# Attention units transposed in pairs, key copies by DMA, GpSimd's results used a step later

## The chip, the cores and the metric

The kernel runs on one core of a Trainium2 chip. The core has five engines that run their own instruction streams and meet at semaphores: TensorE (matrix products; PE in the profile, PEld for its weight loads), VectorE (DVE), ScalarE (ACT), GpSimd (POOL) and SyncE (SP, which here only issues DMAs). Data moves between the chip's memory (HBM) and the core's memory (SBUF) by DMA; results of TensorE land in PSUM, in banks of 128 x 512 floats.

The metric is the time of one execution on the device in microseconds (us), the median of several runs.

## The reference: what is computed

One layer of an encoder block for 1024 tokens of width 1024.

```
h = x @ w_in                                  # 1024 x 1024 @ 1024 x 3328
q_a,k_a,v_a,z_a,q_b,k_b,v_b,z_b = split(h)
y_a = neighborhood_attention(q_a,k_a,v_a)     # 8 heads, grid 16 x 64, window 8 x 16, learned bias
y_b = windowed_gqa_with_sink(rotary(q_b), rotary(k_b), v_b, sink)   # 8 query heads, 2 key heads, |i-j| <= 128
mixed = concat(y_a * silu(z_a), y_b * silu(z_b))
out = layer_norm(2**0.25 * x + mixed @ w_out)
```

Each head has width 64. Both attentions are a softmax over a small window: scores, exponential, division by the sum, weighted sum of the values.

## The kernel before

Float32 accuracy is made of half-precision matmuls: every operand is split into a high and a low float16 part, and a product is three matmuls (high x high, low x high, high x low). ScalarE makes the high part, VectorE or GpSimd the difference.

**Stages.** A prologue computes the values v and the first six column groups of h. The attention loop follows, and at its end the output product with w_out and the layer norm.

**The attention loop.** There are 128 units of work, each one block of 128 queries of one head: units 0 to 63 belong to group b (a 128-query block of one of 8 heads against up to three key blocks), units 64 to 127 to group a (a tile of the grid against three key pieces). Step i of the loop emits, for unit i, the two score matmuls (`stage_qk`, L816 and L817), the bias, minimum and scale on VectorE (L826) and the exponential on ScalarE (`stage_exp`, L842). For unit i - 1 it emits `stage_tr`: ScalarE writes the high part of the probabilities (L852) and VectorE the low part (L853) into a `split` tile, and SP issues a DMA that transposes it, block by block of 128 x 128, into a `tr` tile (L856). Three key pieces with two parts make 6 blocks; the first and the last query block of a head of group b have two key pieces and 4 blocks. Every four units make a group, whose weighted sums with the values (PV, `stage_pv`, L881) stand at step 4q + 9 for group q, so 5 steps after the transpose of its last unit was emitted. `stage_on` divides by the sums (L890), `stage_ot` transposes the result back (L901).

**What fills TensorE.** Between these the loop pumps matmuls of the remaining projections (`project`, L379) and, later, of the output product (L1031), spread over the steps by the table `FILL_AT`.

**Order and queues.** The order of the loop's instructions is written out by hand. Work that the projections bring along goes into four queues, one for each of ScalarE, VectorE, GpSimd and SP (`enq`, L155 on); each step takes a few operations from each (`pop`). An operation may be taken when the operations that it depends on were emitted at an earlier step; `lag` asks for further steps between, two for a DMA. `need` emits what is still queued when a stage must have it. Weight halves pass through such a chain: load (L188, SP), high part (L199, ScalarE), scale and difference (L204 and L205, GpSimd). Queries of group b are rotated (`rope`: L311, L312, then L313 to L315 on GpSimd) and then cast (L259, ScalarE) and subtracted (L265, GpSimd). Keys are cast (L257), subtracted (L263), and their high and low rows are copied to the other half of the partitions (`split_k`, L295, GpSimd), so that each head's keys stand twice, against the high and the low rows of the queries.

**Buffers.** Six `split` tiles are used in turn; the `tr` pool has nine. The score banks in PSUM are four.

Of the kernel before, what the change touches and what calls it, by code (L numbers as in the profile page):

```python
# [9 lines left out]
F16 = mybir.dt.float16  # L10
I32 = mybir.dt.int32
BF16 = mybir.dt.bfloat16
AF = mybir.ActivationFunctionType
# [11 lines left out]
PSCALE = 2.0 ** 14  # L25
MSCALE = 2.0 ** -44
QSCALE = 2.0 ** -15
LTT, LPP, BP, BH, BR, ND, NA, NX, F1 = 1, 6, 2, 9, 5, 1, 1, 6, 0.2
NSPLIT, NP = 6, 2
ORDER = ["zb0", "z0", "zb1", "kb", "qb0", "z1", "qb1", "zb2", "qb2", "k0", "qb3", "zb3", "q0", "k1", "q1",  # L30
         "k2", "q2", "z2", "k3", "q3", "z3"]
NPRO = 6
# [11 lines left out]
WO_TAG = ("wor", "wor", "raw", "raw") + ("wr",) * 5 + ("wor", "wor", "raw", "raw", "raw", "wr", "wr")  # L44
WO_SCAN = ((9, 2), (12, 4), (10, 6), (13, 8), (14, 10), (15, 13))
WO_PREV = {15: ("s", 9), 0: ("s", 10), 1: ("s", 15), 2: ("s", 12), 3: ("s", 13), 11: ("s", 14)}
WO_SCALE = 55
M_AT = [105, 112, 118, 120]
WO_AT = [67, 71, 75, 79, 84, 88, 93, 98]
WO_LD = [16, 22, 19, 25, 36, 39, 42, 45, 48, 112, 116, 28, 130, 130, 130, 130]  # L50
# [11 lines left out]
def hybrid_block(ctx, tc, xT, x, wt, wv, wo, bias, sink, gain, lbias, cos, sin, bmask, out):  # L62
    nc = tc.nc
# [19 lines left out]
    def big_tile(name, shape=(128, 2, 512), dt=F32R):  # L83
        n = taken[0]
        taken[0] += 1
        tag = "big" if n < 8 or 16 <= n < 24 or n >= 32 + NS else "big2"
        return big.tile(list(shape), dt, tag=tag, name=name)

    xh, xl, x16h, x16l = {}, {}, {}, {}
    for half in range(2):  # L90
        for k in range(KT):
            t = big_tile(f"x{half}{k}", dt=F32 if half else F32R)
# [51 lines left out]
    clock = {"step": None}  # L144

    class Op:
        def __init__(self, eng, fn, deps, prio):
            self.eng, self.fn, self.deps, self.step = eng, fn, [d for d in deps if d is not None], None
            self.prio, self.born, self.lag = prio, clock["step"], 2 if eng == "sp" else 0

        def emit(self):
            self.fn()
# [2 lines left out]
    def enq(eng, fn, *deps, prio=1, after=0):  # L155
        op = Op(eng, fn, deps, prio)
        if clock["step"] is not None:
            queues[eng].append(op)
        elif after:
            events.setdefault(ran[0] + after, []).append(op.emit)  # L160
        else:
            op.emit()
        return op
# [3 lines left out]
    def pop(eng, n, top=1, same=False):  # L167
        q = queues[eng]
        ready = [op for op in q if op.prio <= top and all(
            d.step is not None and d.step + d.lag < clock["step"] + (same and op.prio == 0 and d.eng == "act") for d in op.deps)]  # L170
        for op in sorted(ready, key=lambda op: op.prio)[:n]:
            q.remove(op)
            op.emit()
# [80 lines left out]
    def split_hl(h, l, src, scaled, eng):  # L254
        def hi():
            if scaled:
                nc.scalar.activation(h(), src, AF.Copy, scale=QSCALE)  # L257
            else:
                nc.scalar.copy(h(), src)  # L259

        def lo():
            if scaled:
                nc.vector.scalar_tensor_tensor(l(), src, QSCALE, h(), op0=ALU.mult, op1=ALU.subtract)  # L263
            else:
                (nc.gpsimd if eng == "pool" else nc.vector).tensor_sub(l(), src, h())  # L265

        return hi, lo
# [15 lines left out]
    def split_k(p, half, src, dep=None):  # L283
        sl = slice(512 * half, 512 * half + 512)
        ops = []
        prio = 0 if dep is None else 1
        eng = "pool" if dep and clock["step"] is not None else "dve"
        for j in range(2):
            a, o = slice(64 * j, 64 * j + 64), slice(64 - 64 * j, 128 - 64 * j)
            hi, lo = split_hl(lambda j=j, a=a: own("kh", p, j)[a, sl], lambda j=j, a=a: own("kl", p, j)[a, sl],  # L290
                              src[a], dep is None, eng)

            def dup_(w, j=j, a=a, o=o):
                t = own(w, p, j)
                nc.gpsimd.tensor_copy(t[o, sl], t[a, sl])  # L295

            o1 = enq("act", hi, dep, prio=prio, after=28 if dep else 0)
            o2 = enq(eng, lo, o1, prio=prio, after=32 if dep else 0)
            ops.append(o2)
            dup = [enq("pool", lambda d=dup_: d("kh"), o1, after=32 if dep else 0),  # L300
                   enq("pool", lambda d=dup_: d("kl"), o2, after=36 if dep else 0)]
            stk_ops.setdefault((p, j, half), []).extend(dup)
        return ops

# [420 lines left out]
    ap = actx.enter_context(tc.tile_pool(name="ap", bufs=3, reuse_waits="tile"))  # L725
# [28 lines left out]
        return us  # L754

    units = unit_list()
    split = [ap.tile([128, 3, 2, 128], F16, name=f"split{i}", bufs=1) for i in range(NSPLIT)]
    sns = [ap.tile([128, 388], F32, name=f"sn{i}", bufs=1) for i in range(2)]
    for t in split:
        nc.gpsimd.memset(t, 0.0)  # L760
# [2 lines left out]
    st = {}  # L763
    on = {}

    def geom(u):
        g, p, j, t, _ = u
        if g == "a":
            b, half = t
            w = WINW[b]  # L770
            return NKEY[b], [4 * w] * 3
        lo, hi = max(t - 1, 0), min(t + 2, 8)
        return 128 * (hi - lo), [128] * (hi - lo)
# [69 lines left out]
        st[u, "p"] = pt  # L843

    def stage_tr(u):
        g, p, j, t, _ = u
        n, ch = geom(u)
        pt = st.pop((u, "p"))
        c, m = ch[0], len(ch)
        hl = split[units.index(u) % NSPLIT]  # L850
        src = pt[:, :n].rearrange("p (k c) -> p k c", c=c)
        nc.scalar.activation(hl[:, :m, 0, :c], src, AF.Copy, scale=PSCALE)  # L852
        nc.vector.scalar_tensor_tensor(hl[:, :m, 1, :c], src, PSCALE, hl[:, :m, 0, :c],  # L853
                                       op0=ALU.mult, op1=ALU.subtract)
        tr = ap.tile([128, 6, 128], F16, tag="tr", name="tr", bufs=BH)
        nc.sync.dma_start(tr[:, :2 * m, :], hl[:, :m].rearrange("p k i c -> p (k i c)"), transpose=True)  # L856
        st[u, "tr"] = tr

    def quad(q):
        g, p, j, t, _ = units[4 * q]  # L860
# [320 lines left out]
    for i in range(-LD, NU + LO):  # L1181
        if 0 <= i + LD < NU:
            stage_load(units[i + LD], i)
        if i < 0:
            continue
        clock["step"] = i
        per, h = divmod(i, 16)
        bulk["step"] = i
        if i in VA_AT:
            gather_v(0, VA_AT.index(i))  # L1190
        for n, at_ in WO_SCAN:
            if at_ == i:
                load_ops["wo", ("s", n)] = enq("sp", lambda n=n: wo_load(n, True), wo_ops.get(WO_PREV.get(n) if n == 15 else None))
                wo_scan(n, True)
        for n in range(16):
            if WO_LD[n] == i:
                load_ops["wo", n] = enq("sp", lambda n=n: wo_load(n), wo_ops.get(WO_PREV.get(n) if n < 15 else None),
                                        wo_ops.get({9: 0, 10: 1, 12: 2, 13: 3, 14: 4, 15: 5}.get(n)),
                                        w_ops.get(17 + n if 4 <= n <= 8 else None))
                if n < 9 or n == 11:  # L1200
                    wo_scan(n)
        if i == WO_SCALE:
            wo_scale()
        for n in range(len(WO_AT)):
            if WO_AT[n] == i:
                wo_split(n)
        if i == 131:
            enq("sp", gain_load, *m_ops[4])
        if i in M_AT:
            m_queue(4 + M_AT.index(i))  # L1210
        if bulk["last"] != i or (queues["sp"] and i - queues["sp"][0].born > 2):
            pop("sp", 1 if i < 118 else 3)
        if i < NU:
            u = units[i]
            if u[3] in (0, 4):
                need(*stk_ops[f"b{u[1]}", u[2], u[3] // 4])
            if u[3] == (0, 0):
                need(*stk_ops[u[1], u[2], 0], *stk_ops[u[1], u[2], 1])
            stage_qk(u)
        q, m = divmod(i - LP - 3, 4)  # L1220
        if i >= Q30 + 2:
            q, m = (NU // 4 - 2, i - Q30 - 2) if i < Q30 + 4 else divmod(i - LP - 3, 4)
        elif i >= Q30:
            q, m = -1, 0
        if m == 0 and 0 <= q - 1 < NU // 4:
            stage_ot(q - 1)
        if m == 0 and 0 <= q < NU // 4:
            stage_pv(q)
        if i > Z3_END:
            pop("dve", 1, 0)  # L1230
        if 0 <= i - LT < NU:
            stage_tr(units[i - LT])
        pop("act", 1, 0)
        pump_to(i + F1)
        if 0 <= q < NU // 4:
            g, p, j, h = quad(q)
            if g == "a" and p < 3 and (j, h, m) in VA_STEP:
                gather_v(p + 1, VA_STEP.index((j, h, m)))
        if m == 1 and 0 <= q < NU // 4:
            stage_on(q)  # L1240
        pop("dve", ND if i < M_AT[1] else 2, same=True)
        if i < NU:
            stage_exp(units[i])
        pop("act", NA if i < M_AT[0] and len(queues["act"]) < 5 else 2)
        pop("pool", NP)
        pump_to(i + 1)
# [78 lines left out]
```

## Time and profile before

| | |
|---|---|
| median of 3 runs | 446.06 us (445.18 to 448.8) |
| the profiled execution, its own time | 446.49 us |
| its span from first to last instruction | 444.7 us |
| TensorE busy | 437.5 us, 98% |
| VectorE, ScalarE busy | 344.2 us (77%), 308.3 us (69%) |
| GpSimd busy | 221.6 us (50%) |
| DMA moved | 81.39 MB, 183 GB/s on average |
| transposes issued by SP | 128, between 126.1 and 361.3 us |

Rows of the profile name an engine, a source line, an operation and the tiles that it writes and reads; "x128" counts instructions, and a time behind "<-" is idle time and what ended it. In a list of waits the columns are the total, the number of times and the longest, in us. In a timeline the first two columns are the start in us and the length in us.

### The profile page before, as it was taken

To read this page: it belongs to the slowest core of one execution; us is meant where nothing else is said; L and a number is where in the kernel's file an instruction comes from. 1 tells how busy PE (TensorE), PEld (TensorE's weight loads), DVE (VectorE), ACT (ScalarE), POOL (GpSimd) and SP (SyncE) were. 2 spreads that over 40 slices of the span, in tenths; PEclk is the share of its full clock that TensorE was granted. 3 is DMA by queue.
4 is the path that set the end of the run, shared out by engine and by line. 5 is a ranking of instruction groups with operands and counts; after the bars stand their busy time and mean duration, and the time that the engine had idled before them with its cause. 6 is when DMAs were issued, how large, how long until landed. Compare 5 with 4: busy or idle time off the path is not lost.

```text
span 444.7 us, 9505 instructions
## 1 busy us (share of the span) xinstructions
PE 437.5 (98%) x3289; PEld 255.5 (57%) x3289; DVE 344.2 (77%) x849; ACT 308.3 (69%) x700; POOL 221.6 (50%) x235
## 2 busy tenths in 40 slices
PE   9999999999999999999999999999999999999994
PEld 8997754444445565655565655656555654444453
DVE  5978967438986898887988888888878837589944
ACT  5759789766499988887868887888778946302401
POOL 0110074646839558866506767765574405205740
PEclk9999999999999999999999999999999999999997
DMA  8921469984659999587978899998999998103612
GB/s 272 390 91 60 145 235 339 336 292 169 213 127 214 206 190 181 98 162 143 164 127 175 169 182 180 213 170 213 192 204 253 167 172 347 55 0 102 232 69 72
DMA packets 133841, 81.39 MB, mean 183 GB/s; under 512 B 101280, under 2 KB 113440, under 8 KB 133536
## 3 DMA queue, kind: packets, MB, share of 16 engines
q1 hardware_dynamic: 133648, 80.64, 75.4%
q8 instruction: 26, 0.43, 0.4%
q14 instruction: 23, 0.19, 0.2%
q10 hardware_dynamic: 144, 0.13, 0.1%
HBM read 50.34 MB, written 9.96 MB: 136 GB/s over the span
## 4 chain that ended last, share of the span: by engine, by line
PE 91%; DMA 3%; POOL 3%; DVE 1%; issue 1%; ACT 1%; SPq 0%; POOLq 0%; DVEq 0%; ACTq 0%
PE ps_pj L379 44%; PE ps_s L1031 9%; PE ps_s L486 6%; PE ps_t L881 6%; PE ps_pj L1031 5%; PE ps_t L1031 5%; PE ps_s L816 4%; PE ps_s L817 4%; PE ps_pj L486 3%; PE ps_t L486 3%; DMA bias<-in_bias 3%; PE ps_t L901 1%; POOL wl L205 1%; PE ps_t L412 1%; POOL ks L295 1%
## 5 line engine op out<-in xcount | busy, mean ns | idle before, releaser
L379 PE MATMUL ps_pj<-xf,wh 128*128 128x512 f16 x672 | 202.1, 379 | 0.1
L379 PE MATMUL ps_pj<-xf,wl 128*128 128x512 f16 x336 | 127.3, 379 | 0.0
L379 PEld LDWEIGHTS <-wh 128*128 128x128 f16 x672 | 63.7, 98 | 60.4 <-DVE ks L263 0.5
L842 ACT ACTIVATE ps_s<-sn,nm 128x385 f32<-128x385 f32 (+3 forms) x128 | 70.1, 548 | 25.1 <-DVE nm L826 24.6
L853 DVE SCALAR_TENSOR_TENSOR split<-ps_s,split 128x384 f16<-128x384 f32 (+2 forms) x128 | 65.7, 513 | 27.5 <-ACT split L852 25.9
L1031 PEld LDWEIGHTS <-m 128*128 128x128 f16 x432 | 40.0, 98 | 41.1 <-DVE m L939 0.2
L852 ACT ACTIVATE split<-ps_s 128x384 f16<-128x384 f32 (+2 forms) x128 | 57.8, 452 | 2.5 <-DMA tr<-split 0.2
L204 POOL TENSOR_SCALAR wr<-wr,wsc 128x512 f32<-128x512 f32 x26 | 20.6, 791 | 68.1 <-ACT wh L199 61.6
L379 PEld LDWEIGHTS <-wl 128*128 128x128 f16 x336 | 32.9, 98 | 37.4
L826 DVE CUSTOM_DVE_ANT_0 sn<-ps_s,bm,nsk 128x384 f32<-128x384 f32 (+1 forms) x64 | 40.7, 636 | 2.0 <-PE ps_s L817 1.7
L1031 PE MATMUL ps_s<-wo,m 128*128 128x512 f16 (+1 forms) x192 | 40.8, 366 | 0.0
L816 PE MATMUL ps_s<-ks,qs 128*128 128x384 f16 (+4 forms) x128 | 39.2, 306 | 0.3 <-DVE qs L263 0.3
L817 PE MATMUL ps_s<-ks,qs 128*128 128x384 f16 (+4 forms) x128 | 39.2, 306 | 0.0
L826 DVE CUSTOM_DVE_ANT_0 sn<-ps_s,bias,sg 128x264 f32<-128x264 f32 (+1 forms) x64 | 35.0, 547 | 4.5 <-issue 1.5
L881 PEld LDWEIGHTS <-tr 128*128 128x128 f16 (+1 forms) x1104 | 36.6, 98 | 2.2
L205 POOL TENSOR_TENSOR wl<-wr,wh 128x512 f16<-128x512 f32 x26 | 32.7, 1257 | 2.2
L788 POOL TENSOR_SCALAR bias<-bias,rsg 128x552 f32<-128x552 f32 (+1 forms) x24 | 19.1, 797 | 23.8 <-DMA bias<-in_bias 22.6
L295 POOL COPY ks<-ks 64x512 f16<-64x512 f16 x40 | 26.0, 661 | 7.1 <-DVE ks L263 2.8
L1086 ACT ACTIVATE sd<-mv,eps 128x1 f32<-128x1 f32 x8 | 2.4, 295 | 36.5 <-DVE mv L1084 35.2
L1031 PE MATMUL ps_pj<-wo,m 128*128 128x512 f16 (+1 forms) x144 | 26.2, 326 | 0.0
L1130 POOL TENSOR_TENSOR xr<-xr,gb 128x512 f32<-128x512 f32 x7 | 9.8, 1396 | 32.4 <-ACT xr L1127 32.4
L842 ACT ACTIVATION_READ_ACCUMULATOR ps_s<-sn,nm 128x1 f32 x128 | 24.4, 190 | 0.0
(188 smaller groups left out, 813.8 us busy)
## 6 DMA issues: line engine op xcount, KB each, us to landing
ws<-in_wt SPq DMA_DIRECT2D x15, 512.0 KB, 5.9
wr<-in_wt SPq DMA_DIRECT2D x26, 256.0 KB, 3.6
wor<-in_wo SPq DMA_DIRECT2D x22, 256.0 KB, 3.5
bias<-in_bias SPq DMA_DIRECT2D x16, 276.0 KB, 3.3
xr<-in_x SPq DMA_DIRECT2D x8, 512.0 KB, 9.6
out<-xr SPq DMA_DIRECT2D x15, 256.0 KB, 2.1
bias<-in_bias SPq DMA_DIRECT2D x8, 368.0 KB, 3.8
wvraw<-in_wv SPq DMA_DIRECT2D x9, 320.0 KB, 5.8
```

The lines of the kernel that those rows point to most:

```text
L205: nc.gpsimd.tensor_sub(l, raw, h)
L295: nc.gpsimd.tensor_copy(t[o, sl], t[a, sl])
L379: nc.tensor.matmul(ps, a[:, k % 4, :], mv, start=(k == 0 and i == 0), stop=(k == KT - 1 and i == 2))
L486: nc.tensor.matmul(ps[:, :320], lh[:, ts], rh[:, cs], start=(k == ko[0] and i == 0), stop=(k == ko[-1] and i == 2))
L816: nc.tensor.matmul(ps[:, :m], q, sl[0], start=True, stop=False)
L817: nc.tensor.matmul(ps[:, :m], q, sl[1], start=False, stop=True)
L826: nc.vector.tensor_tensor_reduce(sn[:, :m], ps[:, :m], bias_t, sg[:, c:c + 1], init, op0=ALU.add, op1=ALU.min, accum_out=nm)
L842: nc.scalar.activation(pt[:, :m], sn[:, :m], AF.Exp, bias=nm, scale=-1.0, accum_out=sm[:, k:k + 1])
L852: nc.scalar.activation(hl[:, :m, 0, :c], src, AF.Copy, scale=PSCALE)
L853: nc.vector.scalar_tensor_tensor(hl[:, :m, 1, :c], src, PSCALE, hl[:, :m, 0, :c], op0=ALU.mult, op1=ALU.subtract)
L881: nc.tensor.matmul(ps[:, HD * m:HD * m + HD], a, b_, start=(i == 0), stop=(i == len(mms) - 1))
L1031: nc.tensor.matmul(ps, lh[:, ts], rh[:, cs], start=(e == EO[0] and i == 0), stop=(e == EO[-1] and i == 2))
```

## The change

Three edits are made together, with a few constants.

1. **Pairs.** `stage_tr` still makes the high and low parts for one unit at a time, but writes both units of a pair into one tile of 12 blocks, the larger unit first. The transpose is issued once for the pair, at the odd unit. The `split` tiles become three of double size (they were six), and the `tr` pool has four tiles of 12 blocks (it had nine of 6).
2. **Keys.** Inside the loop, the copies of keys to the other half of the partitions are DMAs issued by SP, and no longer GpSimd copies. The keys `k0` to `k3` of group a are projected inside the loop; those of group b are projected in the prologue and keep the GpSimd copies.
3. **GpSimd's lag.** An operation that depends on a GpSimd operation waits one step more before it may be emitted.

The scale of w_out is computed at step 60 (it was 55), and up to two SP operations are taken in a step (it was one).

```
-LTT, LPP, BP, BH, BR, ND, NA, NX, F1 = 1, 6, 2, 9, 5, 1, 1, 6, 0.2
-NSPLIT, NP = 6, 2
+LTT, LPP, BP, BH, BR, ND, NA, NX, F1 = 1, 6, 2, 4, 5, 1, 1, 6, 0.2
+NSPLIT, NP = 3, 2
...
-WO_SCALE = 55
+WO_SCALE = 60
...
-            self.prio, self.born, self.lag = prio, clock["step"], 2 if eng == "sp" else 0
+            self.prio, self.born, self.lag = prio, clock["step"], {"sp": 2, "pool": 1}.get(eng, 0)
...
+        live = clock["step"] is not None
+        to = "sp" if live else "pool"
...
-                nc.gpsimd.tensor_copy(t[o, sl], t[a, sl])
+                if live:
+                    nc.sync.dma_start(t[o, sl], t[a, sl])
+                else:
+                    nc.gpsimd.tensor_copy(t[o, sl], t[a, sl])
...
-            dup = [enq("pool", lambda d=dup_: d("kh"), o1, after=32 if dep else 0),
-                   enq("pool", lambda d=dup_: d("kl"), o2, after=36 if dep else 0)]
+            dup = [enq(to, lambda d=dup_: d("kh"), o1, after=32 if dep else 0),
+                   enq(to, lambda d=dup_: d("kl"), o2, after=36 if dep else 0)]
...
-    split = [ap.tile([128, 3, 2, 128], F16, name=f"split{i}", bufs=1) for i in range(NSPLIT)]
+    split = [ap.tile([128, 6, 2, 128], F16, name=f"split{i}", bufs=1) for i in range(NSPLIT)]
...
     def stage_tr(u):
-        g, p, j, t, _ = u
-        n, ch = geom(u)
+        i = units.index(u)
         pt = st.pop((u, "p"))
+        sizes = [geom(units[2 * (i // 2) + j]) for j in range(2)]
+        first = 0 if sizes[0][0] >= sizes[1][0] else 1
+        n, ch = sizes[i % 2]
         c, m = ch[0], len(ch)
-        hl = split[units.index(u) % NSPLIT]
+        o = 0 if i % 2 == first else 3
+        hl = split[i // 2 % NSPLIT]
         src = pt[:, :n].rearrange("p (k c) -> p k c", c=c)
-        nc.scalar.activation(hl[:, :m, 0, :c], src, AF.Copy, scale=PSCALE)
-        nc.vector.scalar_tensor_tensor(hl[:, :m, 1, :c], src, PSCALE, hl[:, :m, 0, :c],
+        nc.scalar.activation(hl[:, o:o + m, 0, :c], src, AF.Copy, scale=PSCALE)
+        nc.vector.scalar_tensor_tensor(hl[:, o:o + m, 1, :c], src, PSCALE, hl[:, o:o + m, 0, :c],
                                        op0=ALU.mult, op1=ALU.subtract)
-        tr = ap.tile([128, 6, 128], F16, tag="tr", name="tr", bufs=BH)
-        nc.sync.dma_start(tr[:, :2 * m, :], hl[:, :m].rearrange("p k i c -> p (k i c)"), transpose=True)
-        st[u, "tr"] = tr
+        if i % 2 == 0:
+            return
+        tr = ap.tile([128, 12, 128], F16, tag="tr", name="tr", bufs=BH)
+        w = 2 * (len(sizes[0][1]) + len(sizes[1][1]))
+        nc.sync.dma_start(tr[:, :w, :], hl.rearrange("p k i c -> p (k i c)")[:, :128 * w], transpose=True)
+        for j in range(2):
+            st[units[i - 1 + j], "tr"] = tr[:, 0 if j == first else 6:]
...
-            pop("sp", 1 if i < 118 else 3)
+            pop("sp", 2 if i < 118 else 3)
```

## The prediction

> **What bounds the kernel now.** I read the page first, then TensorE's waits, then the table of windows over the attention stage, then the chain.
>
> ```profile
> span 444.7 us, 9505 instructions
> PE 437.5 (98%) x3289; PEld 255.5 (57%) x3289; DVE 344.2 (77%) x849; ACT 308.3 (69%) x700; POOL 221.6 (50%) x235
> PEclk9999999999999999999999999999999999999997
> ...
> PE ps_t L1111 <- ACT dr L1109: 1.8, 1, 1.8
> PE ps_t L412 <- DVE warm L127: 1.0, 1, 1.0
> PE ps_s L816 <- DVE qs L263: 0.3, 1, 0.3
> ...
> PEld L816 <- DVE qs L263: 0.7, 1, 0.7
> PEld L379 <- DVE ks L263: 0.5, 1, 0.5
> ...
> 68.72 10.38 PE ps_pj L379 x48
> 158.74 1.29 PE ps_pj L379 x6
> ...
> sum 240.00, PE 239.64 PEld 137.44 DVE 197.44 ACT 198.00 POOL 146.49; mean PE 47.93 PEld 27.49 DVE 39.49 ACT 39.60 POOL 29.30
> ```
>
> TensorE is busy 98% of the span and waits three times in all. The last row sums five windows that cover 122 to 362 us, the stage that the diff touches: TensorE is idle there for 0.36 us. Busy need not mean full pace, so the two rows of the chain compare pace: 48 projection matmuls in 10.38 us before the stage, 6 in 1.29 us inside it, 0.216 us each in both. The attention stage is a TensorE stream with no holes. Its instructions are the same after the change: in the built order of both kernels TensorE differs in one place, the small matmul of the W_out scale (L971), moved five steps. So **the change can win at most about 1.2 us**, the 0.7 and 0.5 us that TensorE's weight loads wait in the stage, and everything else it does is a question of what new wait it makes.
>
> **The change part by part.**
>
> *Fewer, larger transposes (SP).*
>
> ```profile
> L856 SPq DMA_TRANSPOSE tr<-split x128: 1188/1212/2615, 126.1 to 361.3; - x128
> DMA to landing us min/median/max: 2.5/3.4/6.2
> 137.20 1.21 SPq L856 DMA_TRANSPOSE tr<-split  x1
> 197.10 1.19 SPq L856 DMA_TRANSPOSE tr<-split  x1
> ```
>
> 128 issues of 1.21 us become 64. The 1.21 us row is a 6-block transpose, the 1.19 us row a 4-block one (an edge unit of group b): two blocks add 0.02 us, so I take 1.27 us for 12 blocks. SP sheds 128 x 1.21 - 64 x 1.27 = 74 us of issue time. TensorE never waits for SP as such, so this is worth nothing directly. What matters is when the transposed tile of the last pair of a group of four units lands against the PV matmuls (L881) that read it. Landing after the issue ends is 3.4 - 1.21 = 2.2 us at the median. Bounds for 12 blocks, from issue to landing: 3.4 us if the second half hides, 1.27 + 2 x 2.2 = 5.7 us if everything behind the issue doubles. The nearest case is two transposes issued back to back, 1.21 + 3.4 = 4.6 us from the first issue; I take 4.5 us. SP now arrives free, so I add only 0.1 us between VectorE's last write (L853) and the issue.
>
> The room for it is the time from the end of L853 of a group's fourth unit to the first PV matmul of its third unit, the first that needs the late pair. The tightest and the loosest of the 32 groups:
>
> ```profile
> 234.90 0.56 DVE L853 SCALAR_TENSOR_TENSOR split<-ps_s,split 128x384 f16<-128x384 f32 x1 [0.24 <-ACT split L852]
> 239.04 0.75 PE L881 MATMUL ps_t<-vb,tr 128*128 128x64 f16 x20
> ...
> 315.70 0.46 DVE L853 SCALAR_TENSOR_TENSOR split<-ps_s,split 128x288 f16<-128x288 f32 x1 [0.36 <-ACT split L852]
> 324.48 1.21 PE L881 MATMUL ps_t<-va,tr 128*128 128x64 f16 x36
> ```
>
> PV takes 0.029 us a matmul here (1.05 us for 36 in the chain), and 15 to 18 of them stand before the third unit. So the room is 239.04 + 0.44 - 235.46 = 4.0 us at the tightest and 324.48 + 0.52 - 316.16 = 8.8 us at the loosest. Read in the same way, 2 of 32 groups have under 5.0 us, 5 under 5.5, 10 under 6.0; the shortfalls add up to 0.4 us for a landing 4.5 us after L853, 1.1 us for 5.0, 3.5 us for 5.6 and 6.5 us for 6.0. At 4.6 us, with single transposes late by contention as they are now (maximum 6.2 against 3.4), I put **0.7 us** on TensorE, between 0 and 3.5.
>
> Buffers: three pair tiles replace six split tiles, four pair tiles replace nine tr tiles. ScalarE (L852) rewrites a pair tile five steps after its transpose is issued instead of six. 128 units between 126.1 and 361.3 us make a step 1.85 us, so the room is about 9 us less the lag of VectorE, against 4.6. A miss would hold ScalarE and not TensorE at once. I cost it at 0.
>
> *Key copies.* Only those of the projected keys k0 to k3 move; kb's eight are made before the attention loop and stay on GpSimd.
>
> ```profile
> L295 POOL COPY ks<-ks 64x512 f16<-64x512 f16 x32 | 19.0, 608 | 5.5 <-DVE ks L263 2.8 <-ACT ks L257 1.5
> ...
> out<-xr ACTq DMA_DIRECT2D x1, 128.0 KB, 2.0
> xr<-in_x SPq DMA_DIRECT2D x8, 512.0 KB, 9.6
> ```
>
> GpSimd sheds 19.0 us. The 32 copies become DMAs of 64 KB. No such copy inside SBUF is in the trace; I bound its landing by 2.0 and 9.6 us, the shortest and longest medians of the DMA list, and take 3 us, near the smaller transfers. In the built order the latest, k3's, are issued at steps 106 and 107, and its first reader is the score matmul of step 112: at least 5 x 1.85 = 9.3 us. Hidden, 0; without that cover it would be one stall of some microseconds for each k. On SP they stand before a transpose that waits for later VectorE work anyway.
>
> *GpSimd's results a step later.* An operation that depends on a GpSimd one is now emitted one step later. In the built order this moves weight loads (L188) by one step, which keep several steps before their split, and the chain of the rotated queries: GpSimd L313 to L315, cast on ScalarE (L259), difference on GpSimd (L265), read by the score matmul (L816). For qb1 and qb2 at least three steps are left. **For qb3's second half they are not.** Its first head is read at step 52. Before, its cast is emitted at step 47 and L265 at step 48; after, at steps 50 and 51. The rows of before around it:
>
> ```profile
> 210.49 0.60 ACT L259 CAST qs<-rp_raw 64x512 f16<-64x512 f32 x1
> 211.88 0.61 ACT L259 CAST qs<-rp_raw 64x512 f16<-64x512 f32 x1
> 215.10 0.58 ACT L842 ACTIVATE ps_s<-sn,nm 128x385 f32<-128x385 f32 x1
> 215.60 0.19 ACT L842 ACTIVATION_READ_ACCUMULATOR ps_s<-sn,nm 128x1 f32 x1
> ...
> 211.16 1.16 POOL L265 TENSOR_TENSOR qs<-rp_raw,qs 64x512 f16<-64x512 f32 x1 [2.75 <-ACT qs L259]
> 215.00 0.69 POOL L204 TENSOR_SCALAR ws<-ws,wsc 128x512 f32<-128x512 f32 x1 [1.27 <-ACT wh L199]
> 215.77 1.16 POOL L205 TENSOR_TENSOR wl<-ws,wh 128x512 f16<-128x512 f32 x1
> ...
> 215.66 0.33 PE L816 MATMUL ps_s<-ks,qs 128*128 128x384 f16 x1
> ```
>
> Step 52's score matmul starts at 215.66 (the 53rd row of L816); L265 was done at 212.32, 3.3 us ahead. After the change the cast stands behind the exponential of unit 50 (215.10, done with its accumulator at 215.79), so it ends at 215.79 + 0.61 = 216.4. L265 stands behind the weight split L204 and L205, which ends at 216.93; it would end at 216.93 + 1.16 = 218.1. TensorE, which takes its instructions in order, waits 218.1 - 215.66 = 2.4 us, and behind L816 are queued that step's projection matmuls, the very work that fills it. The other bound: both casts (0.60 and 0.61) are gone from in front of unit 50 on ScalarE, and if the whole row of work there moves up by them, the wait is 2.4 - 1.2 = 1.2 us. VectorE also sits in that row, so I take the middle: **1.8 us**. Nothing gives it back, as TensorE has no idle time to shorten later; at best the lag of VectorE behind TensorE shrinks, which loosens the tight group at 235 us.
>
> *The rest.* The W_out scale five steps later has its scans emitted nine steps earlier and its first user seven steps later: 0. Two SP operations a step instead of one only bring loads forward: 0.
>
> **Sum.** 1.8 + 0.7 = +2.5 us, TensorE's total wait rising from 3 to some 5.5 us. The profiled execution took 446.49 us around its span of 444.7; the median of the runs is 446.06, and a copy of the profiled one would give 449.0. Against the median I predict **448.6 us**, 0.6% slower, which is inside the 1% that a measurement of this kernel can tell from no change.
>
> **Rivals.**
>
> *Nothing shows.* ScalarE and GpSimd run ahead by more than I allow and the pairs land in time. For it: SP and GpSimd shed 74 and 19 us, and 22 of the 32 groups have 6 us or more. Against it: three steps less for a chain that had 3.3 us. Time: 444.9 to 446.8, likeliest 446.1; the lower end is 446.06 less the 1.2 us that TensorE has to give.
>
> *Late pairs, slower by more than 1%.* Place: the PV matmuls of each group. Price: if a 12-block transpose costs issue time by its blocks, 2 x 1.21 = 2.4 us, it lands 4.6 + 1.15 = 5.7 us after L853, and the shortfalls come to about 4 us; with the 1.8 us of step 52 that is +5.9, about 452. It decides once the landing passes 5.6 us. For it: present landings reach 6.2 us when loads compete. Against it: 1.19 us for 4 blocks and 1.21 for 6, and a stall that lets VectorE catch up widens the next room. [...]
>
> *A gain beyond 1%.* This would need 4.5 us of TensorE time, and the stage holds 1.2. That the change does not do what it says I rule out: the built order shows 64 transposes and 32 copies on SP.
>
> **How the numbers follow.** Forecast case (one stall at step 52 and perhaps a few late groups, 446.8 to 450.5): 0.58. Nothing shows: 0.25. Late pairs or another systematic wait: 0.16. Gain beyond 1%: 0.01. Hence faster 0.01, same 0.83, slower 0.16. The range reaches from the lower part of the second case to the upper bounds of both unknown prices, 446.06 + 2.4 + 3.5 = 452.0, drawn in to 451.8, since both at once is unlikely, and down to 445.4: 445.4 to 451.8.
>
> **What would show it.** Among TensorE's waits a new row L816 (or its weight load) on GpSimd's qs L265, once, 1.2 to 2.4 us, near 215 us. PV waits (L881) on the transpose DMA, few, under 1 us each. The transposes: 64 of about 1.27 us, landing median 4 to 5 us. GpSimd busy near 202 us, SP's transposes near 82 us in sum. The prediction is wrong if step 52 shows no wait, if L881 waits on most groups, or if TensorE waits for a key copy.

## The result: 1.2% slower

The changed kernel takes 451.65 us (median of 6 runs, 450.99 to 452.07) against 445.91 us of the kernel before beside it: a ratio of 1.0117, with a 95% interval of 1.0088 to 1.0145. The forecast was 448.6, in a range that reached to 451.8, so the measured time lies 0.15 us inside its upper end. The sign was right and the size was not: the change costs 5.2 us by the ratio and 5.7 by the medians, where I had summed 2.5.

The profiled execution took 451.8 us around a span of 450.0, 5.3 us more than the span before. These are lines of the page of the changed kernel: the span, the busy time of the engines, and TensorE's granted clock in 40 slices.

```profile
span 450.0 us, 9258 instructions
...
PE 438.7 (97%) x3289; PEld 255.9 (57%) x3289; DVE 346.9 (77%) x849; ACT 308.3 (69%) x700; POOL 201.6 (45%) x200
...
PEclk9999999999999999999899999999999999999999
```

GpSimd sheds 20 us and TensorE is still the bound. One slice of the clock, the 20th, shows less than full speed, and no slice of the kernel before did so in the attention stage. (The lines of the kernel have moved: L816/L817 are now L821/L822, L853 is L861, L842 is L847, L881 is L893, L313 to L315 are L318 to L320, L341 is L346, L379 is L384.) Next, what TensorE waited for in the changed kernel (sum in us, times, longest):

```profile
PE ps_s L821 <- POOL qs L265: 3.0, 1, 3.0
PE ps_t L1123 <- ACT dr L1121: 1.8, 1, 1.8
PE ps_t L417 <- DVE warm L127: 1.0, 1, 1.0
PE ps_s L821 <- DVE split L861: 0.9, 1, 0.9
PE ps_s L821 <- DVE qs L263: 0.4, 1, 0.4
PE ps_t L893 <- DMA tr<-split: 0.2, 1, 0.2
```

The rows on L1121, L127 and L263 (0.3 us then) were there before. New are 3.0 us on GpSimd's L265, the wait that I had foreseen at step 52; 0.9 us on VectorE's L861 at step 49, which I had not; and 0.2 us on a transpose. The first two in TensorE's order of time, and a stretch behind them; and then the table of windows around it (busy us of PE, PEld, DVE, ACT, POOL; granted clock; DMA share; GB/s):

```profile
210.49 0.32 PE L821 MATMUL ps_s<-ks,qs 128*128 128x384 f16 x1 [0.92 <-DVE split L861]
...
219.46 0.34 PE L821 MATMUL ps_s<-ks,qs 128*128 128x384 f16 x1 [2.99 <-POOL qs L265]
220.47 1.06 PE L384 MATMUL ps_pj<-xf,wh 128*128 128x512 f16 x2
...
224.47 0.60 PE L384 MATMUL ps_pj<-xf,wh 128*128 128x512 f16 x2
```

```profile
220.40:223.80 3.40, 3.40 (x21) 2.19 (x20) 1.74 (x6) 2.73 (x6) 2.37 (x3) 0.50 0.73 163
223.80:234.00 10.20, 10.20 (x106) 6.14 (x104) 8.60 (x23) 6.18 (x18) 0.00 (x0) 1.00 0.55 106
```

From 0.9 us behind the end of the 2.99 us wait the granted clock is 0.50 for 3.4 us, and two projection matmuls take 1.06 us where they take 0.60 four microseconds later. Half of 3.4 us, 1.7 us, is lost there. So the span's +5.3 us comes from four pieces: 0.9 + 3.0 + 1.7 + 0.2 = 5.8. Against them stand a hole of 0.3 us at 241 us in the kernel before, which is gone, and a first score matmul that starts 0.4 us sooner in this trace (121.3 us, before 121.8).

**Where the 0.9 us comes from, and part of the 3.0.** GpSimd's, ScalarE's and VectorE's order of time in the changed kernel, and then ScalarE's and GpSimd's in the kernel before:

```profile
204.21 2.38 POOL L265 TENSOR_TENSOR qs<-rp_raw,qs 64x512 f16<-64x512 f32 x2
206.66 1.26 POOL L318 TENSOR_TENSOR rp_raw<-rp_raw,cos 128x512 f32<-128x512 f32 x1
...
218.25 1.15 POOL L265 TENSOR_TENSOR qs<-rp_raw,qs 64x512 f16<-64x512 f32 x1
```

```profile
207.96 0.69 ACT L346 ACTIVATE z<-ps_pj,invt 128x512 f32<-128x512 f32 x1 [3.22 <-POOL rp_raw L318]
...
216.42 0.57 ACT L847 ACTIVATE ps_s<-sn,nm 128x385 f32<-128x385 f32 x1
217.02 0.60 ACT L259 CAST qs<-rp_raw 64x512 f16<-64x512 f32 x1
```

```profile
208.68 0.69 DVE L347 SCALAR_TENSOR_TENSOR z<-z,ps_pj 128x512 f32<-128x512 f32 x1 [3.35 <-ACT z L346]
```

```profile
205.87 0.69 ACT L341 ACTIVATE z<-ps_pj,invt 128x512 f32<-128x512 f32 x1 [1.75 <-POOL rp_raw L313]
```

```profile
199.91 2.38 POOL L265 TENSOR_TENSOR qs<-rp_raw,qs 64x512 f16<-64x512 f32 x2
...
204.57 1.27 POOL L313 TENSOR_TENSOR rp_raw<-rp_raw,cos 128x512 f32<-128x512 f32 x1
```

ScalarE's tanh of zb3 (L346) writes a tile that lies in the slot of the cosine table (ZTAG gives zb3 the tag "zc", under which the table was loaded). It must therefore wait for the last multiplication by that table, L318 of qb3's second half. It did so before, for 1.75 us. In the kernel before, two query differences (L265, 2.38 us) are done at 202.3 us, and a weight split stands between them and the multiplication. In the changed kernel the lag brings them a step later, between that split and L318, so that L318 starts at 206.66 and not at 204.57. ScalarE stands for 3.22 us, VectorE behind it for 3.35 us, the release of a score bank is late, and TensorE waits 0.92 us. ScalarE is still behind at step 50: the exponential of unit 50, ahead of the cast that step 52 needs, starts at 216.42 and no longer at 215.10.

The DMAs, from the views of the two lines (issue time in ns: min/median/max; first and last start in us):

```profile
L867 SPq DMA_TRANSPOSE tr<-split x64: 1253/1446/3644, 126.9 to 364.0; - x64
...
DMA to landing us min/median/max: 3.4/4.1/6.6
...
L298 SPq DMA_DIRECT2D ks<-ks x32: 461/547/2120, 174.8 to 331.9; - x32
...
DMA to landing us min/median/max: 1.9/3.3/5.1
```

A paired transpose is issued in 1.45 us and lands in 4.1 us at the median; a key copy lands in 3.3 us, and no wait of TensorE names one.

### The profile page after: what moved, and what is told of

The parts are those of the page before. It is cut to its first block, busy times and chain, and to the rows that moved or that the text cites. A ratio compares the mean times of both kernels' runs of the same rounds, so it can differ in the third digit from the quotient of the medians.

```text
span 450.0 us, 9258 instructions
## 1 busy us (share of the span) xinstructions
PE 438.7 (97%) x3289; PEld 255.9 (57%) x3289; DVE 346.9 (77%) x849; ACT 308.3 (69%) x700; POOL 201.6 (45%) x200
## 4 chain that ended last, share of the span: by engine, by line
PE 91%; issue 2%; POOL 2%; DVE 2%; ACT 2%; DMA 1%; ACTq 0%; POOLq 0%
PE ps_pj L384 44%; PE ps_s L1043 9%; PE ps_t L893 7%; PE ps_s L491 6%; PE ps_pj L1043 5%; PE ps_t L1043 5%; PE ps_s L821 4%; PE ps_s L822 4%; PE ps_pj L491 3%; PE ps_t L491 3%; PE ps_t L913 2%; DMA tr<-split 1%; PE ps_t L417 1%; POOL qs L265 1%; ACT ps_s L847 0%
## 5 line engine op out<-in xcount | busy, mean ns | idle before, releaser
L384 PE MATMUL ps_pj<-xf,wh 128*128 128x512 f16 x672 | 202.6, 380 | 0.0
L384 PE MATMUL ps_pj<-xf,wl 128*128 128x512 f16 x336 | 127.7, 380 | 0.0
L384 PEld LDWEIGHTS <-wh 128*128 128x128 f16 x672 | 63.8, 98 | 60.1 <-issue 0.2
L847 ACT ACTIVATE ps_s<-sn,nm 128x385 f32<-128x385 f32 (+3 forms) x128 | 70.2, 548 | 30.5 <-DVE nm L831 29.9
L861 DVE SCALAR_TENSOR_TENSOR split<-ps_s,split 128x384 f16<-128x384 f32 (+2 forms) x128 | 65.7, 513 | 28.0 <-ACT split L860 27.2
L384 PEld LDWEIGHTS <-wl 128*128 128x128 f16 x336 | 32.9, 98 | 37.6 <-issue 0.3
L821 PE MATMUL ps_s<-ks,qs 128*128 128x384 f16 (+4 forms) x128 | 39.4, 308 | 4.3 <-POOL qs L265 3.0
L822 PE MATMUL ps_s<-ks,qs 128*128 128x384 f16 (+4 forms) x128 | 39.4, 308 | 0.0
L893 PEld LDWEIGHTS <-tr 128*128 128x128 f16 (+1 forms) x1104 | 37.0, 98 | 2.5 <-DMA tr<-split 0.3
L847 ACT ACTIVATION_READ_ACCUMULATOR ps_s<-sn,nm 128x1 f32 x128 | 24.4, 190 | 0.0
L821 PEld LDWEIGHTS <-qs 128*128 128x128 f16 x128 | 12.6, 98 | 19.4 <-POOL qs L265 3.5
```

The source lines that it names most:

```text
L384: nc.tensor.matmul(ps, a[:, k % 4, :], mv, start=(k == 0 and i == 0), stop=(k == KT - 1 and i == 2))
L821: nc.tensor.matmul(ps[:, :m], q, sl[0], start=True, stop=False)
L822: nc.tensor.matmul(ps[:, :m], q, sl[1], start=False, stop=True)
L847: nc.scalar.activation(pt[:, :m], sn[:, :m], AF.Exp, bias=nm, scale=-1.0, accum_out=sm[:, k:k + 1])
L861: nc.vector.scalar_tensor_tensor(hl[:, o:o + m, 1, :c], src, PSCALE, hl[:, o:o + m, 0, :c], op0=ALU.mult, op1=ALU.subtract)
L893: nc.tensor.matmul(ps[:, HD * m:HD * m + HD], a, b_, start=(i == 0), stop=(i == len(mms) - 1))
```

## The experiments

Ratios are to the kernel before, with 95% intervals; it took 445.9 to 446.7 us beside the experiments.

### One part at a time

**The lag taken out of the whole change:**

```diff
-            self.prio, self.born, self.lag = prio, clock["step"], {"sp": 2, "pool": 1}.get(eng, 0)
+            self.prio, self.born, self.lag = prio, clock["step"], 2 if eng == "sp" else 0
```

> The changed kernel with GpSimd's lag taken back (pairs and key DMAs stay). Theory A, the late query: the lag alone makes the wait of step 52 and the half clock after it, so both go, TensorE's wait on qs L265 is gone from the list, the clock stays at 1.00 through the stage and the time is 445.9 us, between 445.2 and 446.8 (ratio to before 0.998 to 1.002). Theory B, late pairs: the transposes of 12 blocks cost most of it, and the time stays at 449 or above (ratio 1.007 or more).

Measured: 449.45 us, ratio 1.0078 (1.0059 to 1.0098). The wait on L265 is gone and so is the half clock, yet 3 us stay: the time is the one that theory B gave, though not by late pairs, as the run with the pairs alone shows below. ScalarE's wait on the cosine multiplication is 1.7 us again. TensorE's new waits are small and come to under 1 us in the view of waits; the longest is this:

```profile
PE ps_s L821 <- DVE split L861: 0.4, 1, 0.4
```

So the lag causes the large wait, and without it the other parts cost 3 us by something else. What that is became the main question.

**The lag alone**, put into the kernel before:

```diff
-            self.prio, self.born, self.lag = prio, clock["step"], 2 if eng == "sp" else 0
+            self.prio, self.born, self.lag = prio, clock["step"], {"sp": 2, "pool": 1}.get(eng, 0)
```

> The kernel before with GpSimd's lag of one step alone. In the built order the casts of qb3's second half stand behind the exponentials of units 50 and 52 as in the changed kernel, and those of qb2's second half behind 35 and 36, though unit 36 is the first to read them. Theory A: two waits of TensorE on qs L265, near steps 36 and 52, each of 2 to 4 us and, where it reaches 3 us, with half the clock for 3.4 us behind it (1.7 us): 450 to 457 us, likeliest 454. Theory B: the lag costs under 2 us, so 448 or less.

Measured: 458.03 us, ratio 1.0263 (1.0238 to 1.0288), above even the range that I gave. TensorE's waits and the windows behind them:

```profile
PE ps_s L816 <- POOL qs L265: 7.0, 2, 4.0
...
PE ps_s L816 <- DVE split L853: 0.9, 1, 0.9
```

```profile
190.90:194.30 3.40, 3.40 (x24) 2.26 (x23) 1.84 (x6) 2.90 (x7) 2.73 (x3) 0.50 0.32 63
225.10:231.90 6.80, 5.91 (x38) 3.60 (x39) 3.58 (x9) 4.50 (x11) 3.83 (x4) 0.50 0.81 173
```

Two waits on L265, 4.0 us at step 36 and 3.0 us at step 52, and half clock for 10.2 us behind them, 3.4 behind the first and 6.8 behind the second. 7.0 + 0.9 + 5.1 = 13.0, against 12.6 us of span; 0.9 us of the second half clock still lie in the wait, so the sum is 0.5 too high. The full change doesn't have the wait at step 36. In the trace of the lag alone GpSimd still makes the key copies, and two of them and two query differences stand ahead of the addition that ends the rotation before step 36; that the copies alone make this second chain late was not tested.

**The pairs alone:** the changed kernel with the lag, the key copies, the second SP operation and the step of the W_out scale set back.

```diff
-        to = "sp" if live else "pool"
+        to = "pool"
...
-            pop("sp", 2 if i < 118 else 3)
+            pop("sp", 1 if i < 118 else 3)
```

> The kernel before with the paired transposes and their buffers alone (keys on GpSimd, no lag). Theory A: a wait or two of PV on the transposes, under 1 us in sum: 446.2 us, between 445.5 and 447.2. Theory B: 449 or above, with PV (the line of the weighted sums) waiting on the transposes in several groups.

Measured: 446.19 us, ratio 1.0005 (0.9991 to 1.0018), and no matmul of PV waits. The pairs cost nothing and bring nothing, and the late pairs of theory B do not occur.

**The key copies alone:** in the kernel before, the copies by DMA and two SP operations a step, single transposes as they were.

```diff
-                nc.gpsimd.tensor_copy(t[o, sl], t[a, sl])
+                if live:
+                    nc.sync.dma_start(t[o, sl], t[a, sl])
+                else:
+                    nc.gpsimd.tensor_copy(t[o, sl], t[a, sl])
...
-            pop("sp", 1 if i < 118 else 3)
+            pop("sp", 2 if i < 118 else 3)
```

> The kernel before with the key copies as DMAs and two SP operations a step alone. Theory A: GpSimd sheds 19 us, TensorE never waits for a key copy: 445.8 us, between 445.2 and 446.6. Rival: 32 more DMAs in SP's queue delay single transposes or bias loads, some waits of 1 us and more: 447 or above.

Measured: 459.13 us, ratio 1.0273 (1.0247 to 1.03). I had put the likeliest time at 445.8 us; the rival, transposes that are delayed by 32 more DMAs on SP, came true and costs far more than the 447 us named for it. TensorE's new wait, and SP's order of time ahead of the worst of it:

```profile
PE ps_t L886 <- DMA tr<-split: 7.1, 6, 3.8
```

```profile
284.43 1.18 SPq L298 DMA_DIRECT2D ks<-ks  x2
285.71 1.23 SPq L861 DMA_TRANSPOSE tr<-split  x1
287.04 0.53 SPq L745 DMA_DIRECT2D va<-vwin  x1
287.67 0.45 SPq L789 DMA_DIRECT2D bias<-in_bias  x1
288.17 2.39 SPq L298 DMA_DIRECT2D ks<-ks  x2
```

A step takes 1.85 us. A single transpose (1.23), two copies (1.18) and a value or bias load are already more than SP issues in one, so transposes come late, TensorE waits up to 3.8 us for one, and the half clock follows (6.8 and 3.4 us of it in this trace). The copies come two to a step because of the second SP operation; how much of the cost is that operation's was not measured. With pairs a step has 0.7 us of transposes on SP and not 1.2, and pairs and copies together cost 3 us (the run without the lag): **the pairs are what pays for the key copies.** The parts don't add: pairs 0, copies with the second SP operation +12.2 us, lag +11.7 us (from the ratios), all together +5.2.

### What makes the half clock

The clock had not been in my sum. In the kernel before I planted GpSimd work (5, 8 or 12 operations on a small tile) at step 54, with a matmul on that tile ahead of the step's score matmul, so that TensorE waits once for a chosen time. This adds work and leaves none out.

```diff
+        if units.index(u) == 54:
+            for _ in range(5):
+                nc.gpsimd.tensor_scalar(warm, warm, 1.0, 1.0, op0=ALU.mult, op1=ALU.mult)
+            nc.tensor.matmul(ps[:, :128], warm, warm, start=True, stop=True)
         nc.tensor.matmul(ps[:, :m], q, sl[0], start=True, stop=False)
```

> The kernel before with a planted wait: at step 54 TensorE first runs one small matmul on a tile that GpSimd has passed through 5 extra operations of 128x128, queued behind its weight split. By the slope of the scaling operations (0.69 us for 512 columns, 0.80 us on the mean of 552 and 736) one takes about 0.33 us, so TensorE waits about 1.7 us, between 1.2 and 2.2. If a wait costs its own length and the clock falls only behind a longer one: 446 + 1.7 = 447.6 us and a clock of 1.00. If any wait over 1 us brings the half clock: 449.3.

> The same with 8 operations: a wait of about 2.7 us (2.2 to 3.2). Without the half clock 448.6 us; with 3.4 us of it behind the wait 450.3. I expect the runs on either side, since the changed kernel shows it behind a wait of 3.0 us.

> The same with 12 operations: a wait of about 4.0 us (3.5 to 4.6). With half the clock for 3.4 us behind it, 1.7 us lost: 446 + 4.0 + 1.7 = 451.7 us; if the wait costs only its length 450.0.

Measured: 448.4 us (ratio 1.0043, 1.0017 to 1.0068), 450.6 (1.0093, 1.0066 to 1.012) and 453.01 (1.0144, 1.0113 to 1.0174). The planted wait (from the view of waits), then a window behind it, for the three kernels in turn:

```profile
PE ps_s L819 <- POOL warm L818: 1.7, 1, 1.7
```

```profile
217.00:227.00 10.00, 8.29 (x76) 4.90 (x75) 8.59 (x26) 6.57 (x18) 3.31 (x7) 1.00 0.71 150
```

```profile
PE ps_s L819 <- POOL warm L818: 2.8, 1, 2.8
```

```profile
223.50:227.00 3.50, 3.50 (x12) 1.39 (x11) 2.83 (x9) 1.20 (x3) 0.00 (x0) 0.51 0.36 69
```

```profile
PE ps_s L819 <- POOL warm L818: 4.8, 1, 4.8
```

```profile
225.00:228.40 3.40, 2.80 (x8) 1.15 (x9) 1.77 (x6) 1.08 (x3) 0.46 (x2) 0.50 0.00 0
```

The wait of 1.7 us costs about its own length (1.9 us by the ratio) and leaves the clock at 1.00 in this trace, which is of the fastest of ten runs that spread from 446.8 to 450.2. Waits of 2.8 and 4.8 us (I had expected at most 4.6) each bring 3.4 us at 0.50: 2.8 + 1.7 = 4.5 against 4.1 us by the ratio; 4.8 + 1.4 = 6.2 against 6.4, as 0.6 us of that half clock still lie in the wait. So the half clock follows the wait itself, and the price of the 3.0 us wait in the changed kernel is its length and 1.7 us.

These three runs don't fix how long a wait must be. In the run with the key copies alone TensorE waits 0.31 and then 1.32 us for transposes near 358 us, and that is enough:

```profile
359.59 0.45 PE L886 MATMUL ps_t<-va,tr 128*128 128x64 f16 x9 [1.32 <-DMA tr<-split]
```

```profile
359.87:363.28 3.41, 3.41 (x15) 1.33 (x12) 1.21 (x5) 0.78 (x3) 2.52 (x3) 0.50 1.01 213
```

The 1.8 us wait on `dr` near the end has the clock at 0.50 behind it in the kernel before (the wait ends at 439.23 us, the clock is 0.50 from 439.83) and at 1.00 in the changed kernel (the wait ends at 444.85 us, the clock is 1.00 until 449.09, after the last matmul). Where a wait falls seems to count as well. With the lag alone the clock is 0.50 from 190.93 to 194.34 and from 225.06 to 231.89 us; these stretches and the one between them last 3.41, 6.83 and 30.72 us, which is 1, 2 and 9 times 3.413. In the changed kernel it is 0.50 from 220.40 to 223.81 and 1.00 from there to 449.09 us, which is 1 and 66 times 3.413. So in these two traces the changes of the clock lie whole multiples of 3.41 us apart. No run here moves a wait without changing it, so that the place decides was not shown. What the traces show is how long the half clock lasts in the attention loop, 3.4 us, and 6.8 us in one stretch with the lag alone (225.1 to 231.9) and in one with the key copies alone (291.6 to 298.4), and that it came behind one wait of 2.8 us and behind 0.31 and 1.32 us together.

### The cosine table's slot

Is it really the slot that lifts the wait of step 52 to 3 us? The whole change, with the multiplication by the cosine put ahead of other waiting work in GpSimd's queue. In the built order one instruction moves.

```diff
-        o3 = enq(eng, lambda: mul.tensor_mul(raw, raw, tiles["cos"][:, sl]), o2, after=3)
+        o3 = enq(eng, lambda: mul.tensor_mul(raw, raw, tiles["cos"][:, sl]), o2, after=3, prio=0)
```

> The whole change, with one edit: the multiplication by the cosine table (GpSimd, L318) goes ahead of waiting work in GpSimd's queue; in the built order one instruction moves, for qb3's second half, ahead of a weight split and two query differences (L204, L205, two L265). Theory: zb3 lies in the cosine table's slot, so ScalarE's tanh and VectorE after it stand until that multiplication is done; with it earlier the 0.92 us wait at 210 us goes, and ScalarE and VectorE come into steps 50 to 52 some 1.5 to 3 us earlier, so that the wait on L265 at step 52 shrinks from 3.0 to below 2 us and the half clock behind it goes too: 451.65 - 0.9 - 1 - 1.7 = 448.0, between 447.3 and 449.5. Rival (the slot has no part in it; the wait on L265 is set by GpSimd's own order): only the 0.9 us goes at most, 450.7 to 451.7, wait 3 us and half clock as they were.

Measured: 447.46 us, ratio 1.0033 (1.0021 to 1.0045), a little better than the theory's 448.0. GpSimd's row that moved, ScalarE's tanh and cast, and TensorE at step 52:

```profile
203.07 1.27 POOL L318 TENSOR_TENSOR rp_raw<-rp_raw,cos 128x512 f32<-128x512 f32 x1 [1.98 <-DVE rp_sw L317]
```

```profile
205.90 0.69 ACT L346 ACTIVATE z<-ps_pj,invt 128x512 f32<-128x512 f32 x1
...
215.00 0.60 ACT L259 CAST qs<-rp_raw 64x512 f16<-64x512 f32 x1
```

```profile
217.40 0.34 PE L821 MATMUL ps_s<-ks,qs 128*128 128x384 f16 x1 [0.86 <-POOL qs L265]
```

The tanh no longer waits, the cast is done 2.0 us sooner, the wait at 210 us is gone, the wait of step 52 falls from 2.99 to 0.86 us, and the clock stays at 1.00. The rotation's own end is not what helps: in the changed kernel it was done at 210.5 us, 6.5 us before the cast. The gain is 0.9 + 2.1 + 1.7 = 4.7 us; the times differ by 4.2. **The place of one instruction on GpSimd decides about three quarters of what the change costs.**

### The 3 us that stay without the lag

**The lag only where the reader is SP** (weight loads), to see whether those loads make the difference:

```diff
-            self.prio, self.born, self.lag = prio, clock["step"], {"sp": 2, "pool": 1}.get(eng, 0)
+            self.prio, self.born, self.lag = prio, clock["step"], 2 if eng == "sp" else 0
...
-            d.step is not None and d.step + d.lag < clock["step"] + (same and op.prio == 0 and d.eng == "act") for d in op.deps)]
+            d.step is not None and d.step + (1 if eng == "sp" and d.eng == "pool" else d.lag) < clock["step"] + (same and op.prio == 0 and d.eng == "act") for d in op.deps)]
```

> The changed kernel, with the extra step behind GpSimd kept only for what SP issues (weight loads) and taken from the compute queues. Theory A: the same as without any lag, 445.9 us (445.2 to 446.8). If the weight loads' extra step itself did harm, 447 or above.

Measured: 449.21 us, ratio 1.0063 (1.0042 to 1.0085): 3 us above what I expected and the same as without any lag, so it is not the order of the loads.

**The W_out scale.** Its VectorE operations fall at 235 us, where the first holes are. Undone beside the lag (as shown), and, the other way round, set to 60 alone in the kernel before:

```diff
-WO_SCALE = 60
+WO_SCALE = 55
```

> The changed kernel with two of its edits undone: GpSimd's results are used as in the kernel before, and the W_out scale stands at step 55 again. Pairs, key copies by DMA and two SP operations a step stay. With the lag alone undone it took 449.45 us against 446.22, by many TensorE holes of 0.2 to 0.5 us between 228 and 335 us. Theory W (the scale's five VectorE operations, 0.9 us, fall at 235 us into the stretch in which VectorE is furthest behind, and the holes start there): 446.2 to 447.5, holes gone before 260 us. Theory K (the key copies and the second SP operation of a step make the holes): 449 again. If both share it: about 448.

> The kernel before with the W_out scale at step 60 and nothing else changed. Theory W: 0.7 to 2 us slower (446.9 to 448), with TensorE holes between 235 and 260 us that the kernel before does not have. Theory K: as before, within 0.3 us (446.1).

Measured: 449.56 us (ratio 1.0087, 1.0063 to 1.011) and 446.28 us (1.0004, 0.9991 to 1.0017). The scale has no part in it. In the first of these traces two late transposes make TensorE wait 1.3 us.

**GpSimd's order.** I then measured the lead in each trace: the time from the end of VectorE's last reading of a score bank (L853, later L861) to the score matmul that uses the bank again four steps on. At about 0.05 us TensorE is waiting. The smaller of the leads at steps k and k + 1, in us:

| k | before | pairs alone | no lag | changed kernel | cosine first | no lag, addition first |
|---|---|---|---|---|---|---|
| 16 | 0.33 | 0.32 | 0.05 | 1.15 | 1.16 | 0.75 |
| 36 | 2.31 | 2.31 | 1.00 | 1.75 | 1.76 | 2.20 |
| 52 | 1.49 | 1.48 | 0.34 | 4.33 | 3.98 | 1.49 |
| 66 | 0.22 | 0.30 | 0.05 | 1.36 | 1.35 | 0.24 |
| 88 | 0.87 | 0.87 | 0.11 | 0.89 | 0.89 | 0.05 |

The kernel before passes step 66 with 0.2 us to spare: TensorE was the only engine that looked busy, but VectorE was 0.2 us from making it wait there. Without the lag 1.3 us of lead are lost by step 36, and at step 66 none is left. GpSimd's and ScalarE's order of time in the kernel without the lag show where:

```profile
176.08 1.27 POOL L319 TENSOR_TENSOR rp_sw<-rp_sw,sin 128x512 f32<-128x512 f32 x1
177.42 1.16 POOL L265 TENSOR_TENSOR qs<-rp_raw,qs 64x512 f16<-64x512 f32 x1
178.66 1.27 POOL L320 TENSOR_TENSOR rp_raw<-rp_raw,rp_sw 128x512 f32<-128x512 f32 x1
```

```profile
179.96 0.62 ACT L259 CAST qs<-rp_raw 64x512 f16<-64x512 f32 x1 [1.89 <-POOL rp_raw L320]
```

A query difference has slipped in between the two halves of a rotation. In the kernels with key copies on GpSimd the copies stand in the queue there, and the difference comes after the rotation, as GpSimd's order with the pairs alone shows (L318 is the addition there, L298 the copies):

```profile
176.92 1.27 POOL L318 TENSOR_TENSOR rp_raw<-rp_raw,rp_sw 128x512 f32<-128x512 f32 x1
178.25 1.16 POOL L298 COPY ks<-ks 64x512 f16<-64x512 f16 x2
179.38 1.16 POOL L265 TENSOR_TENSOR qs<-rp_raw,qs 64x512 f16<-64x512 f32 x1
```

With the copies gone the queue is shorter, the difference is taken earlier, and ScalarE stands 1.89 us for the addition. The last run puts the addition first, without the lag; in the built order two instructions move, both on GpSimd.

```diff
-        o5 = enq(eng, lambda: mul.tensor_add(raw, raw, sw), o3, o4, after=4)
+        o5 = enq(eng, lambda: mul.tensor_add(raw, raw, sw), o3, o4, after=4, prio=0)
```

> The changed kernel without the lag (449.5 us against 446.1), with one more edit: the addition that ends a rotation (GpSimd, L320) goes ahead of waiting work in GpSimd's queue. In the built order two instructions move, both on GpSimd: in one half L320 ahead of a weight split (L204, L205), in the other ahead of one query difference (L265). Theory O (with the key copies gone from GpSimd's queue, a query difference slips in between L319 and L320; ScalarE's cast stands 1.9 us at 178 us for it, VectorE loses 1.3 us of its lead over TensorE, the lead is used up at 235 to 243 us, and TensorE's holes there and after are that): the lead is back at 2.3 us at step 36, the holes between 235 and 260 us go, 446.2 to 447.7. Rival S (the key copies and the second SP operation of a step make transposes land late, whatever GpSimd's order): the holes stay, 448.7 to 449.8.

Measured: 448.07 us, ratio 1.0038 (1.0027 to 1.005), between the two theories. The lead is back up to step 66 (last column), and of the three holes between 235 and 243 us one of 0.3 us is left, which the kernel before has too. So GpSimd's order makes 1.3 us of the 3 by the medians, 1.8 by the ratios. The rest is not settled. At step 88 the lead is still used up, and just behind it the trace shows one late transpose as the largest piece:

```profile
287.54 0.70 PE L893 MATMUL ps_t<-va,tr 128*128 128x64 f16 x18 [0.73 <-DMA tr<-split]
```

It lies at the same place as the overload of SP in the run with the copies alone, which speaks for the rival's mechanism as the other share; a run that takes the second SP operation away by itself was not made. The spans differ by 0.9 us from before and the times by 1.7 (ratio) to 1.9 (medians), so the trace doesn't hold all of it. In the changed kernel itself these small holes don't occur: its stall at step 52 lets VectorE catch up to a lead of 4.3 us.

No version here beats the kernel before. The pairs alone equal it, and the best with all parts is 0.3% slower.

## Why the prediction was right or wrong

The range held, and that was luck in part: its upper end was made of 2.4 us at step 52 and 3.5 us for late pairs. Late pairs cost 0.2 us; terms that I had not named, 0.9 and 1.7 us, and a larger wait filled their place.

**Bound and ceiling: right.** TensorE stayed the bound and nothing was gained. What I left out is how close the second engine stood: 0.2 us of lead at step 66. The share of busy time (VectorE 77%) doesn't show that.

**Fewer, larger transposes: mechanism right, the wait put too high.** Issue 1.45 us for the 1.27 assumed; landing 4.1 us at the median for the 4.5 assumed, within its bounds; TensorE's wait 0.2 us where I put 0.7, and none with the pairs alone. The rival "late pairs" fell. The issue time did grow, by 0.24 us at the median, but it did not double as the rival had it: 12 blocks take 1.45 us, two transposes of 6 take 2.4.

**Key copies: the cost of 0 failed as it was argued.** The landing (3.3 us for 3) and its cover were right. But "on SP they stand before a transpose that waits for later VectorE work anyway" holds only beside the pairs; without them the copies and the second SP operation cost 12.2 us. And I counted what leaves GpSimd only as time, not as a change of what its queue takes next.

**The step of GpSimd's results: the place right, the size wrong.** The wait on L265 came once, at step 52, as foreseen: 3.0 us for the 1.8 taken, above the upper bound of 2.4. The step that went wrong is the one that put ScalarE's row where it was or moved it up. It moved down by 1.3 us (the exponential of unit 50 from 215.10 to 216.42), for a reason that I had not looked for: a tile that shares its slot with the cosine table, and L265 in front of the table's last reader. The row of the kernel before with its 1.75 us idle time showed that dependence. Without it the wait is 0.9 us, shorter than the lower bound of 1.2. Two terms were missing altogether: the 0.9 us at step 49 from the same stall, and 1.7 us of half clock. The page of the kernel before held a sign of it: the last digit of its PEclk row is 7, and there the clock is 0.50, from 439.83 us on, behind a wait of 1.8 us.

**The rest.** The W_out scale: 0, confirmed. Two SP operations a step, put at 0: not measured alone, and contained in the run that cost 12.2 us.

**Sum.** 1.8 + 0.7 became 3.0 + 0.9 + 1.7 + 0.2. "Nothing gives it back" was right for the time, and the remark that a stall gives VectorE lead again was right too: that is why the changed kernel has no holes after it.

## What to carry to other kernels

Before an operation is moved by a step, list the tiles that share a slot with its operands, and read for each neighbouring engine how much lead it has at the tightest step, not how busy it is. Taking work off a queue also changes the order of what stays: compare the order on that engine, and look for short operations that now come between the two parts of a chain. Measure parts of a change together and apart before one is dropped; here the lag and the key copies cost 12 us each alone, and with the pairs all three cost 5 us together.

## What the runs showed of the hardware

In these runs a wait of TensorE could cost more than its length: waits of 2.8 and 4.8 us (planted), 3.0 us (the changed kernel) and 4.0 us (the lag alone) had 3.4 us at a clock of 0.50 behind them, up to 1.7 us lost, and another of 3.0 us (the lag alone) had 6.8. A planted wait of 1.7 us had none in its trace, while waits of 0.31 and 1.32 us close together (the key copies alone) had 3.4 us, so the length alone does not decide. The transposes of the changed kernel, most of them of 12 blocks, cost 0.24 us more issue time than those of the kernel before, most of them of 6 (1.45 us against 1.21 us at the median), and the landing grew from 3.4 to 4.1 us.
